# The forget tile in two buffers, loaded one head ahead, and one pool for the weight load buffers and attention's q, k, v rows

## The chip, the core and the metric

The kernel runs on one core of one Trainium2 chip. Its time is the device time of one launch in microseconds (us), as the median of several runs. On the core work TensorE (PE; its weight loads are shown apart as PEld), VectorE (DVE), ScalarE (ACT), GpSimd (POOL) and SyncE (SP), which here issues the transfers.

## What is computed

One layer of an encoder, for a prompt of 1024 rows and eight samples of 16 rows each with 256 cached rows. Width 1024, 8 heads of 64.

```python
x = x + 0.5 * gt1 * _swiglu(_modulate(x, g_ffn1, sh1, sc1), w_up1, w_down1)
# mixer: one projection z = h @ w_in, split into q, k, v, forget logits, u
q = _rms(q.reshape(B, T, N_HEADS, HEAD_DIM), g_q)
k = _rms(k.reshape(B, T, N_HEADS, HEAD_DIM), g_k)
logf = jax.nn.log_sigmoid((fl + b_f).astype(jnp.float32))
F = jnp.cumsum(logf, axis=1)
s = jnp.einsum('bqhd,bkhd->bhqk', q, k) * (HEAD_DIM ** -0.5)
s = s + (F_q[..., :, None] - F_k[..., None, :])      # -inf where k_pos > q_pos
o = softmax(s) @ v
y = jax.nn.silu(_layernorm(_dwconv(u_pad, conv_w, conv_b), conv_ln_g, conv_ln_b))
x = x + gt2 * (jnp.concatenate([o, y], axis=-1) @ w_out)
x = x + 0.5 * gt3 * _swiglu(_modulate(x, g_ffn2, sh3, sc3), w_up2, w_down2)
return _rms(x, g_final), states
```

## The kernel before

The stages follow one another: modulation vectors, first feed-forward block, combined projection, attention, output projection, second feed-forward block. All products are made of float32 values split into a high part `wh`/`hh` and a rest `wl`/`hl`, three matmuls each (lines 447 to 449 in the feed-forward blocks, 843 to 845 in the projection). Weights come in blocks of 512 KB: SP loads a block into a `raw` tile (a ring of 3), ACT casts it to `wh` (line 117), POOL or DVE subtracts for `wl` (line 118). The ring lies in the same pool as `wh` and `wl`, one pool for each stage.

**The projection** (lines 832 to 882) goes over six blocks of 256 columns (`cb` 0 and 1 are v, 2 and 3 are k, 4 and 5 are q) and in each over nine row tiles (`tt`: 8, the samples' rows, then 0 to 7), 24 matmuls into a bank `z` each. For k and q, ACT squares each of the four heads with a sum (line 859, written into a scratch tile `sq` that exists once), takes the root of the sums (line 860), and DVE makes the reciprocal `rr` (line 861). For `cb` 2 to 4 ACT copies the bank to the tile `qkv` (line 867), POOL multiplies it (line 868; for k once more by the gain), and SP stores it to the DRAM tiles `kd` or `qd` (line 875) and to the output; for `cb` 5 DVE multiplies straight out of the bank (line 865). The tiles `qkv` are slots of a ring of 4 (`tmp`), which the forget sums share (`nf`, line 792; `nfs`, line 810). Between the tiles DVE works through the taps of the depthwise convolution (lines 696 to 700).

**Attention** (from line 964) takes eight heads with four stages each, a stage being two query tiles of 128 rows, in the order 0, 2, 1, 3, the scores two stages ahead of the rest. Up to here PE's order is written out; in attention a scheduler sets the order on all engines from the code's order and the buffers. For each head, SP broadcasts a row of forget sums from DRAM to all partitions, tile `nfb`, 128x1024 (line 1214). For each query tile PE makes scores `s` (lines 1143 to 1146), DVE adds `nfb` and takes the minimum (`T`, `st`, line 1149), ACT takes the exponential (line 1150), DVE the reciprocal (line 1151), POOL scales (line 1152). PE transposes `T` into `pT` (line 251), ACT and DVE split that into `ph` and `pl` (lines 1170 and 1171), PE multiplies with the values `Vs` into `po` (line 1178), and DVE, then POOL, take the result through the tile `o32` (`o` in the profile) to `oth` and `otl` (lines 1190 to 1193). For each pair of heads SP loads 512 KB each of q, k and v rows back from DRAM (`qp`, `kp`, `vp`, line 1076); PE transposes them to `qT`, `kT`, and ACT, DVE and POOL make `Qs`, `Kh`, `kl`, `Vs` of them, for the next head's sake a head ahead. The samples' attention is woven in: `room` tiles hold a sample's cached keys and values (loads at lines 982, 985, 986, 996; the mask `sel`; PE's transposes `kTs`).

The forget tile has one buffer, and its load stands at a head's first stage:

```python
            if n % 4 == 0:
                nfb[h] = ap_.tile([P, SEQ], F32, tag="nfb", name="nfb", bufs=1)
                sp.dma_start(nfb[h], nfd[h:h + 1, :].to_broadcast([P, SEQ]))
                pieces = prep(h + 1) if h + 1 < H else []
```

SP issues transfers in the order of its queue: one that waits holds all behind it.

Of the kernel before, what the change touches and what calls it, by code (L numbers as in the profile page):

```python
# [8 lines left out]
F32 = mybir.dt.float32  # L9
# [34 lines left out]
def trunk_layer(  # L44
# [27 lines left out]
    def r32(ap):  # L72
        return ap.bitcast(F32)
# [21 lines left out]
    class Stream:  # L95
# [5 lines left out]
        def dma(self, n):  # L101
            while self.nd < min(n, self.limit):
                src, a, b = self.blocks[self.nd]
                t = self.pool.tile([P, WSL], F32, tag="raw", name="raw", bufs=3)
                v = t[:, :a * b].rearrange("p (a b) -> p a b", b=b)
                sp.dma_start(v, src)
                self.raw[self.nd] = t[:, :a * b]
                self.nd += 1
# [542 lines left out]
    mask_s = up_.tile([TS, H, TS], BF16, name="mask_s")  # L651
    sel = up_.tile([40, H, TS], F32, name="sel")
    qts = up_.tile([P, 4, P], F32, name="qts")
    kts = up_.tile([P, 4, P], F32, name="kts")
    pool_e.memset(mask_s, 0.0)
    pool_e.affine_select(out=mask_s, in_=mask_s, pattern=[[0, H], [1, TS]], compare_op=ALU.is_ge, fill=NEG, base=0, channel_multiplier=-1)
    pool_e.memset(sel, 0.0)
    pool_e.memset(sel[0:8], 1.0)
    pool_e.affine_select(out=sel[0:8], in_=sel[0:8], pattern=[[-1, H], [0, TS]], compare_op=ALU.is_equal, fill=0.0, base=0, channel_multiplier=1)
    for ct in range(4):  # L660
# [161 lines left out]
    def sample_t(cb):  # L822
# [6 lines left out]
        else:  # L829
            act.activation(dst, b[:, :256], AF.Copy, scale=gqc)  # L830

    for cb, (c0, n) in enumerate(QKV):
        i0 = b_qkv + 2 * cb
        w = [ws.take(i0 + kq) for kq in range(2)]
        ws.split(i0 + 4)
        for tt in [8] + list(range(8)):
# [18 lines left out]
            else:  # L855
                sq = up_.tile([P, DH], F32, tag="sq", name="sq", bufs=1)
                rr = up_.tile([P, 4], F32, tag="rr", name="rr", bufs=3)
                for h in range(4):
                    act.activation(sq, b[:, h * DH:(h + 1) * DH], AF.Square, accum_out=rr[:, h:h + 1])
                act.activation(rr, rr, AF.Sqrt, scale=1.0 / DH, bias=eps)  # L860
# [106 lines left out]
    mat, ap_ = open_pool("at", "left")  # L967
    room = [up_.tile([P, 1416], F32, tag=f"u{i}", name=f"room{i}") for i in range(4)]
    kc = room[0][:, :2 * DA].rearrange("p (a n) -> p a n", a=2)
# [9 lines left out]
    sfv = sf.rearrange("p (h t) -> p h t", h=H)  # L979

    def k_load(s):
        sp.dma_start(kc, cache_k[0, s].rearrange("(a p) h d -> p a (h d)", p=P))

# [4 lines left out]
    def s_a(s):  # L988
        if s == 0:
            k_load(0)  # L990
            dve.memset(nf, 1.0)
            pool_e.memset(bd, 0.0)
            pool_e.memset(vn, 0.0)
            pool_e.memset(pts[:, 256:], 0.0)
            dve.tensor_copy(sfv, sel)
        sp.dma_start(nf[0:H, :], nfsd[:, s, :])
# [72 lines left out]

    ld = {}  # L1070

    def a_load(p):
        ts = []
        for nm, src in (("qp", qd), ("kp", kd), ("vp", vd)):
            t = ap_.tile([P, 8, P], F32, tag=nm, name=nm)
            sp.dma_start(t, src[0:SEQ, p * P:(p + 1) * P].rearrange("(i t) n -> t i n", t=P))
            ts.append(t)
        ld[p] = ts

    nfb, Qs, Kh, Vs = {}, {}, {}, {}  # L1080
    a_load(0)
    kl_t = [ap_.tile([P, SEQ], F32R, tag=f"kl{i}", name=f"kl{i}") for i in range(2)]
# [102 lines left out]
    def out(h, j, po):  # L1185
        rows = slice(h % 2 * DH, (h % 2 + 1) * DH)
        t = tp.tile([P, C], F32, tag="rstd", name="ol", bufs=2)[:, :256]
        act.copy(t[:DH], po[DH:])
        o = ap_.tile([P, 256], F32, tag="o32", name="o32", bufs=2)
        dve.tensor_tensor(o[rows], po[:DH], t[:DH], ALU.add)  # L1190
        cols = slice(2 * j * P, (2 * j + 2) * P)
        pool_e.tensor_scalar(oth[rows, h // 2, cols], o[rows], 1.0, 1.0, ALU.mult, ALU.mult)
        pool_e.tensor_sub(otl[rows, h // 2, cols], o[rows], r32(oth[rows, h // 2, cols]))

# [166 lines left out]
```

## Time and profile before

| | |
|---|---|
| median of 3 runs | 2366.07 us (2365.07 to 2369.52) |
| profiled execution, its own time | 2364.53 us |
| its span in the profile | 2362.7 us |
| PE busy | 2300.0 us, 97% |
| DVE busy | 1242.5 us, 53% |
| ACT, POOL busy | 654.3 us, 533.0 us |
| the projection's last q tile leaves DVE | 1202.2 us after the start |
| forget tiles issued, heads 2 to 7 | 1246.65, 1271.56, 1294.86, 1316.33, 1339.17, 1360.93 us |

The profile is of one execution. A row of a timeline reads: start, length, engine, line, operation, out<-in, shape, and in brackets how long the engine was idle ahead of it and what ended that. A row of waits reads: who waited, for whom, us in total, times, the longest. A row of windows reads: from and to, length, then busy time and instructions of PE, PEld, DVE, ACT and POOL, the clock that TensorE was granted (1.00 is full), the share of the DMA engines, GB/s.

### The profile page before, as it was taken

How to read it: one execution, taken by the hardware profiler on the slowest of the kernel's cores; microseconds unless marked ns; L12 is line 12 of the kernel's file. 1: busy time of each engine (PE TensorE's matmuls, PEld its weight loads, DVE VectorE, ACT ScalarE, POOL GpSimd, SP SyncE). 2: the span in 40 equal slices, each digit the busy share in tenths (PEclk: the TensorE clock that was granted, in tenths of full speed). 3: DMA queues.
4: the chain of work that ended last, by engine and by line, in shares of the span. 5: the costliest groups of instructions: out<-in, count | busy, mean ns of one | idle time of the engine just before them, and what ended most of it. 6: DMA issues, size and time to landing. Idle time of an engine off the chain costs nothing.

```text
span 2362.7 us, 34229 instructions
## 1 busy us (share of the span) xinstructions
PE 2300.0 (97%) x13923; PEld 2205.2 (93%) x13923; DVE 1242.5 (53%) x2349; ACT 654.3 (28%) x1426; POOL 533.0 (23%) x423
## 2 busy tenths in 40 slices
PE   7999999999999998999989989999999999999998
PEld 4899999999999998999977779899999999999997
DVE  4542344244423448899978876843443344423445
ACT  4511111111111114314567753421111111111112
POOL 1111111211211211213446640121221221121210
PEclk8999999999999999999999999999999999999999
DMA  9432323311111111124233220111111111111102
GB/s 308 126 105 91 107 90 108 115 46 36 36 55 36 46 45 47 37 72 134 72 123 101 91 90 28 45 54 36 37 54 36 38 52 36 36 54 36 45 19 81
DMA packets 165301, 165.75 MB, mean 70 GB/s; under 512 B 9983, under 2 KB 141995, under 8 KB 162065
## 3 DMA queue, kind: packets, MB, share of 16 engines
q1 hardware_dynamic: 165145, 163.58, 22.3%
q8 instruction: 110, 1.80, 0.3%
q14 instruction: 46, 0.38, 0.1%
HBM read 147.10 MB, written 16.68 MB: 69 GB/s over the span
## 4 chain that ended last, share of the span: by engine, by line
PE 87%; DVE 7%; DMA 2%; ACT 2%; POOL 1%; issue 1%; SPq 0%; DVEq 0%; ACTq 0%; POOLq 0%
PE ub L447 9%; PE ub L448 9%; PE ub L449 9%; PE ua L447 8%; PE ua L448 8%; PE ua L449 8%; PE d L447 8%; PE d L449 8%; PE d L448 8%; PE pa L342 2%; DVE cv L699 2%; DMA nfb<-nfd 1%; PE z L843 1%; PE z L844 1%; PE z L845 1%; PE wo L449 1%
## 5 line engine op out<-in xcount | busy, mean ns | idle before, releaser
L118 POOL TENSOR_TENSOR wl<-raw,wh 128x1024 fp32r<-128x1024 f32 (+1 forms) x152 | 368.3, 2430 | 1592.2 <-ACT wh L117 1490.1
L486 DVE TENSOR_TENSOR g<-ub,sg 128x384 f32<-128x384 f32 x132 | 73.6, 558 | 772.8 <-PE ub L449 760.6
L447 PE MATMUL ub<-hh,wh 128*128 128x384 f32 x1168 | 399.0, 342 | 2.7 <-ACT hh L431 2.7
L448 PE MATMUL ub<-hl,wh 128*128 128x384 f32 x1168 | 397.5, 340 | 1.0 <-DVE hl L432 1.0
L449 PE MATMUL ub<-hh,wl 128*128 128x384 f32 x1168 | 397.3, 340 | 1.2 <-POOL wl L118 1.2
L447 PE MATMUL ua<-hh,wh 128*128 128x384 f32 x1136 | 381.9, 336 | 0.5 <-ACT hh L442 0.5
L448 PE MATMUL ua<-hl,wh 128*128 128x384 f32 x1136 | 379.9, 334 | 0.9 <-DVE hl L432 0.6
L449 PE MATMUL ua<-hh,wl 128*128 128x384 f32 x1136 | 379.9, 334 | 0.0
L117 ACT CAST wh<-raw 128x1024 fp32r<-128x1024 f32 (+1 forms) x160 | 165.8, 1050 | 763.2 <-issue 448.8
L454 DVE SCALAR_TENSOR_TENSOR x<-d,hgate,x 128x384 f32<-128x384 f32 (+1 forms) x528 | 296.1, 571 | 128.5 <-PE d L449 122.8
L447 PE MATMUL d<-gh,wh 128*128 128x384 f32 x1056 | 356.9, 338 | 4.8 <-DVE t L430 4.7
L449 PE MATMUL d<-gh,wl 128*128 128x384 f32 x1056 | 356.8, 338 | 0.0
L448 PE MATMUL d<-gl,wh 128*128 128x384 f32 x1056 | 355.9, 337 | 0.0
L447 PEld LDWEIGHTS ub<-hh,wh 128*128 128x128 f32 x1168 | 221.3, 189 | 13.1 <-issue 5.9
L447 PEld LDWEIGHTS ua<-hh,wh 128*128 128x128 f32 x1136 | 213.3, 188 | 11.8 <-issue 7.5
L448 PEld LDWEIGHTS ub<-hl,wh 128*128 128x128 f32 x1168 | 221.3, 189 | 1.7 <-DVE hl L432 1.7
L449 PEld LDWEIGHTS ub<-hh,wl 128*128 128x128 f32 x1168 | 221.2, 189 | 1.5 <-POOL wl L118 1.5
L448 PEld LDWEIGHTS ua<-hl,wh 128*128 128x128 f32 x1136 | 213.3, 188 | 1.5 <-DVE hl L432 0.9
L449 PEld LDWEIGHTS ua<-hh,wl 128*128 128x128 f32 x1136 | 213.3, 188 | 0.0
L447 PEld LDWEIGHTS d<-gh,wh 128*128 128x128 f32 x1056 | 199.1, 189 | 12.0 <-DVE t L430 5.0
L448 PEld LDWEIGHTS d<-gl,wh 128*128 128x128 f32 x1056 | 198.8, 188 | 0.0
L449 PEld LDWEIGHTS d<-gh,wl 128*128 128x128 f32 x1056 | 198.6, 188 | 0.0
(261 smaller groups left out, 3186.1 us busy)
## 6 DMA issues: line engine op xcount, KB each, us to landing
raw<-in_w_up_dram SPq DMA_DIRECT2D x88, 512.0 KB
araw<-in_w_ada_dram SPq DMA_DIRECT2D x24, 1024.0 KB
raw<-in_w_down_dram SPq DMA_DIRECT2D x44, 512.0 KB
raw<-in_w_in_dram SPq DMA_DIRECT2D x18, 512.0 KB
abulk<-in_w_ada_dram SPq DMA_DIRECT2D x12, 512.0 KB
out_dram<-yo SPq DMA_DIRECT2D x18, 256.0 KB
out_dram<-qkv SPq DMA_DIRECT2D x34, 128.0 KB
xin<-in_x_prompt_dram SPq DMA_DIRECT2D x8, 512.0 KB
```

The costliest lines, as they stand in the source:

```text
L117: act.copy(hi[:, :a * b], raw)
L118: self.sub.tensor_sub(lo[:, :a * b], raw, r32(hi[:, :a * b]))
L342: pe.matmul(pa[32 * i:32 * i + 32, :], lhsT=cst32[:, k, :], rhs=raw, start=first, stop=last)
L447: pe.matmul(out, lhsT=wh, rhs=mh_, start=first, stop=False)
L448: pe.matmul(out, lhsT=wh, rhs=ml_, start=False, stop=False)
L449: pe.matmul(out, lhsT=wl, rhs=mh_, start=False, stop=last)
L454: dve.scalar_tensor_tensor(xs[:, :n], b[:, :n], gate[:, dt, 0:1], xs[:, :n], ALU.mult, ALU.add)
L486: dve.tensor_tensor(g32, pb[:, :C], sg, ALU.mult)
L699: dve.scalar_tensor_tensor(cv if j < CW - 1 else acc[ct][:, :SEQ], u0, w, cv, ALU.mult, ALU.add)
L843: pe.matmul(b[:, :n], lhsT=a_h, rhs=wh, start=kt == 0, stop=False)
L844: pe.matmul(b[:, :n], lhsT=a_h, rhs=wl, start=False, stop=False)
L845: pe.matmul(b[:, :n], lhsT=a_l, rhs=wh, start=False, stop=kt == KD - 1)
```

## The change

The forget tile gets two buffers; head 0's is loaded ahead of the loop, head h+1's at head h's second stage (`nf_load`). The `raw` ring gets a pool of its own that stays open through the kernel, and attention's `qp`, `kp`, `vp` are tiles of that ring; the first pair's loads and the first sample's key load stand after row tile 2 of the projection's last block. The `sq` tile goes: squares are written into the tile's own slot `t`, which the copy or the product then overwrites. `sel`, `cl` and `o32` move into parts of other tiles, `o32` as one tile instead of two. What is in words only: `k_load` and `room[0]` move ahead of the projection loop with `a_load`, and the two instructions on `o32` after the first follow its new name.

```diff
-                t = self.pool.tile([P, WSL], F32, tag="raw", name="raw", bufs=3)
+                t = self.rawp.tile([P, WSL], F32, tag="raw", name="raw", bufs=3)
...
+    mraw, ws.rawp = open_pool("raw", "left")
     mw, wp = open_pool("w1", "left")
...
-    sel = up_.tile([40, H, TS], F32, name="sel")
-    pool_e.memset(sel, 0.0)
-    pool_e.memset(sel[0:8], 1.0)
-    pool_e.affine_select(out=sel[0:8], ...)
...
-    cl = up_.tile([P, PAST // P * NS * H], F32, tag="cl", name="cl")
+    cl = qts[:, 0, :]
...
+    def a_load(p):
+        ts = []
+        for nm, src in (("qp", qd), ("kp", kd), ("vp", vd)):
+            t = ws.rawp.tile([P, WSL], F32, tag="raw", name=nm, bufs=3)[:, :8 * P].rearrange("p (i n) -> p i n", n=P)
+            sp.dma_start(t, src[0:SEQ, p * P:(p + 1) * P].rearrange("(i t) n -> t i n", t=P))
...
-                sq = up_.tile([P, DH], F32, tag="sq", name="sq", bufs=1)
                 rr = up_.tile([P, 4], F32, tag="rr", name="rr", bufs=3)
                 for h in range(4):
-                    act.activation(sq, b[:, h * DH:(h + 1) * DH], AF.Square, accum_out=rr[:, h:h + 1])
+                    act.activation(t[:, h * DH:(h + 1) * DH], b[:, h * DH:(h + 1) * DH], AF.Square, accum_out=rr[:, h:h + 1])
...
+            if cb == 5 and tt == 2:
+                a_load(0)
+                k_load(0)
...
+    sel = room[3][:40, 1280:1280 + P].rearrange("p (h t) -> p h t", h=H)
+    o32 = room[3][:, 2 * P:4 * P]
...
         if s == 0:
-            k_load(0)
...
+            pool_e.memset(sel, 0.0)
+            pool_e.memset(sel[0:8], 1.0)
+            pool_e.affine_select(out=sel[0:8], ...)
...
-            t = ap_.tile([P, 8, P], F32, tag=nm, name=nm)
...
-    a_load(0)
+    def nf_load(h):
+        nfb[h] = ap_.tile([P, SEQ], F32, tag="nfb", name="nfb", bufs=2)
+        sp.dma_start(nfb[h], nfd[h:h + 1, :].to_broadcast([P, SEQ]))
+
+    nf_load(0)
...
-        o = ap_.tile([P, 256], F32, tag="o32", name="o32", bufs=2)
-        dve.tensor_tensor(o[rows], po[:DH], t[:DH], ALU.add)
+        dve.tensor_tensor(o32[rows], po[:DH], t[:DH], ALU.add)
...
             if n % 4 == 0:
-                nfb[h] = ap_.tile([P, SEQ], F32, tag="nfb", name="nfb", bufs=1)
-                sp.dma_start(nfb[h], nfd[h:h + 1, :].to_broadcast([P, SEQ]))
                 pieces = prep(h + 1) if h + 1 < H else []
+            if n % 4 == 1 and h + 1 < H:
+                nf_load(h + 1)
```

The instructions stay the same, but for one row on PE and one on POOL. Three places of the order, a row for each instruction with what it waits for (DMAHW is a transfer landed; x3 is three alike).

SP's queue at the projection's end, before: the q and k rows stand behind seven stores of the last block.

```order
L875 DMA qd<-qkv 128x256 [waits DMAHW7_49,DVE_49]
L1076 DMA qp<-qd 128x8x128 [waits DMAHW0_49]
L1076 DMA kp<-kd 128x8x128 [waits DMAHW1_49]
L875 DMA qd<-qkv 128x256 [waits DMAHW2_49,DVE_49]
L1076 DMA vp<-vd 128x8x128 [waits DMAHW3_49]
L982 DMA room_10605<-in_cache_k_dram 128x2x512 [waits DMAHW4_49,PE_49]
L1214 DMA nfb<-nfd 128x1024 [waits DMAHW5_49]
```

The same place after:

```order
L889 DMA qd<-qkv 128x256 [waits DMAHW6_49,Pool_49]
L835 DMA qp<-qd 128x8x128 [waits DMAHW4_49,DMAHW5_49,DMAHW3_49,DMAHW6_49,DMAHW2_49,DMAHW7_49,DMAHW1_49,DMAHW0_49]
L835 DMA kp<-kd 128x8x128
L835 DMA vp<-vd 128x8x128
L889 DMA qd<-qkv 128x256 [waits DVE_49,Activation_49]
```

The three loads stand ahead of all stores of the last block. Eight rows further on, ahead of that block's last store, the loads of the forget tiles of heads 0 and 1 now stand side by side, and wait for PE.

SP's queue around the load of head 3's forget tile, before (`room` rows are a sample's keys, forget sums, values and new values):

```order
L982 DMA room_10605<-in_cache_k_dram 128x2x512 [waits DMAHW5_49,PE_49]
L996 DMA room_10606<-nfsd 8x272 [waits DMAHW6_49,DMAHW3_49,PE_49]
L1076 DMA kp<-kd 128x8x128 [waits PE_49]
L1076 DMA vp<-vd 128x8x128 [waits Pool_49]
L985 DMA room_10606<-in_cache_v_dram 128x2x512 [waits DMAHW7_49,PE_49]
L1076 DMA qp<-qd 128x8x128 [waits PE_49]
L1214 DMA nfb<-nfd 128x1024 [waits DMAHW0_49,DVE_49]
```

After:

```order
L1001 DMA room_10575<-in_cache_v_dram 128x2x512 [waits DMAHW3_49,PE_49]
L1002 DMA room_10577<-vd 16x512 [waits DMAHW5_49,DMAHW1_49,PE_49]
L1092 DMA nfb<-nfd 128x1024 [waits DMAHW2_49,DVE_49]
L844 DMA room_10331<-in_cache_k_dram 128x2x512 [waits DMAHW6_49,PE_49]
L1014 DMA room_10575<-nfsd 8x272 [waits DMAHW7_49,DMAHW4_49,PE_49]
L835 DMA qp<-qd 128x8x128 [waits PE_49]
L835 DMA kp<-kd 128x8x128 [waits Pool_49]
```

The forget tile's load stood behind the third pair's rows; it now stands ahead of them and of a sample's keys, one head earlier.

ACT in the projection, two tiles of a q block, before:

```order
L859 ACTIVATE sq,rr<-z 128x64 [waits PE_49,Pool_49]
L859 ACTIVATE sq,rr<-z 128x64 [waits Activation_49] x3
L867 COPY qkv<-z 128x256 [waits DMAHW1_49,DMAHW0_49]
L860 ACTIVATE rr<-rr,eps 128x4 [waits Activation_49]
L859 ACTIVATE sq,rr<-z 128x64 [waits PE_49,Pool_49]
L859 ACTIVATE sq,rr<-z 128x64 [waits Activation_49] x3
L867 COPY qkv<-z 128x256 [waits DMAHW4_49,DMAHW2_49]
```

After:

```order
L873 ACTIVATE qkv,rr<-z 128x64 [waits DMAHW3_49,DMAHW0_49,DMAHW4_49,PE_49,Pool_49]
L873 ACTIVATE qkv,rr<-z 128x64 x3
L874 ACTIVATE rr<-rr,eps 128x4 [waits Activation_49]
L881 COPY qkv<-z 128x256
L873 ACTIVATE qkv,rr<-z 128x64 [waits DMAHW1_49,DMAHW2_49,PE_49,Pool_49]
L873 ACTIVATE qkv,rr<-z 128x64 x3
L874 ACTIVATE rr<-rr,eps 128x4 [waits Activation_49]
```

The wait for the slot's stores moved from the copy to the first square, the squares wait no more for one another, and the root now comes ahead of the copy.

More of the change, by code (lines that the diff above doesn't have):

```diff
@@ L656, in trunk_layer @@
     pool_e.affine_select(out=mask_s, in_=mask_s, pattern=[[0, H], [1, TS]], compare_op=ALU.is_ge, fill=NEG, base=0, channel_multiplier=-1)
-    pool_e.memset(sel, 0.0)
-    pool_e.memset(sel[0:8], 1.0)
-    pool_e.affine_select(out=sel[0:8], in_=sel[0:8], pattern=[[-1, H], [0, TS]], compare_op=ALU.is_equal, fill=0.0, base=0, channel_multiplier=1)
     for ct in range(4):
@@ L830, in sample_t, with k_load @@
             act.activation(dst, b[:, :256], AF.Copy, scale=gqc)
+    ld = {}
+    def a_load(p):
[3 more added lines that the diff above has]
+            sp.dma_start(t, src[0:SEQ, p * P:(p + 1) * P].rearrange("(i t) n -> t i n", t=P))
+            ts.append(t)
+        ld[p] = ts
+    room = []
+    def k_load(s):
+        if s == 0:
+            room.append(up_.tile([P, 1416], F32, tag="u0", name="room0"))
+        sp.dma_start(room[0][:, :2 * DA].rearrange("p (a n) -> p a n", a=2),
+                     cache_k[0, s].rearrange("(a p) h d -> p a (h d)", p=P))
     for cb, (c0, n) in enumerate(QKV):
@@ L967, in trunk_layer @@
     mat, ap_ = open_pool("at", "left")
-    room = [up_.tile([P, 1416], F32, tag=f"u{i}", name=f"room{i}") for i in range(4)]
+    room += [up_.tile([P, 1416], F32, tag=f"u{i}", name=f"room{i}") for i in range(1, 4)]
     kc = room[0][:, :2 * DA].rearrange("p (a n) -> p a n", a=2)
@@ L979, in trunk_layer @@
     sfv = sf.rearrange("p (h t) -> p h t", h=H)
-    def k_load(s):
-        sp.dma_start(kc, cache_k[0, s].rearrange("(a p) h d -> p a (h d)", p=P))
+    sel = room[3][:40, 1280:1280 + P].rearrange("p (h t) -> p h t", h=H)
+    o32 = room[3][:, 2 * P:4 * P]
     def v_load(s):
@@ L994, in s_a @@
             pool_e.memset(pts[:, 256:], 0.0)
+            pool_e.memset(sel, 0.0)
+            pool_e.memset(sel[0:8], 1.0)
+            pool_e.affine_select(out=sel[0:8], in_=sel[0:8], pattern=[[-1, H], [0, TS]], compare_op=ALU.is_equal, fill=0.0, base=0, channel_multiplier=1)
             dve.tensor_copy(sfv, sel)
@@ L1067, in sample_to @@
             f(s)
[L1070 to L1074, printed above, removed]
-            t = ap_.tile([P, 8, P], F32, tag=nm, name=nm)
-            sp.dma_start(t, src[0:SEQ, p * P:(p + 1) * P].rearrange("(i t) n -> t i n", t=P))
-            ts.append(t)
-        ld[p] = ts
     nfb, Qs, Kh, Vs = {}, {}, {}, {}
-    a_load(0)
+    def nf_load(h):
+        nfb[h] = ap_.tile([P, SEQ], F32, tag="nfb", name="nfb", bufs=2)
+        sp.dma_start(nfb[h], nfd[h:h + 1, :].to_broadcast([P, SEQ]))
+    nf_load(0)
     kl_t = [ap_.tile([P, SEQ], F32R, tag=f"kl{i}", name=f"kl{i}") for i in range(2)]
@@ L1188, in out @@
         act.copy(t[:DH], po[DH:])
-        o = ap_.tile([P, 256], F32, tag="o32", name="o32", bufs=2)
-        dve.tensor_tensor(o[rows], po[:DH], t[:DH], ALU.add)
+        dve.tensor_tensor(o32[rows], po[:DH], t[:DH], ALU.add)
         cols = slice(2 * j * P, (2 * j + 2) * P)
-        pool_e.tensor_scalar(oth[rows, h // 2, cols], o[rows], 1.0, 1.0, ALU.mult, ALU.mult)
-        pool_e.tensor_sub(otl[rows, h // 2, cols], o[rows], r32(oth[rows, h // 2, cols]))
+        pool_e.tensor_scalar(oth[rows, h // 2, cols], o32[rows], 1.0, 1.0, ALU.mult, ALU.mult)
+        pool_e.tensor_sub(otl[rows, h // 2, cols], o32[rows], r32(oth[rows, h // 2, cols]))
     def flush(n):
@@ L1325, in trunk_layer @@
     close_pool(mw)
+    close_pool(mraw)
     close_pool(mps)
```

## The prediction

> **What bounds the kernel now.** I read the page first: which engine is full, and what the chain of work that ended last consists of.
>
> ```profile
> span 2362.7 us, 34229 instructions
> PE 2300.0 (97%) x13923; PEld 2205.2 (93%) x13923; DVE 1242.5 (53%) x2349; ACT 654.3 (28%) x1426; POOL 533.0 (23%) x423
> PE 87%; DVE 7%; DMA 2%; ACT 2%; POOL 1%; issue 1%; SPq 0%; DVEq 0%; ACTq 0%; POOLq 0%
> PE ub L447 9%; PE ub L448 9%; PE ub L449 9%; PE ua L447 8%; PE ua L448 8%; PE ua L449 8%; PE d L447 8%; PE d L449 8%; PE d L448 8%; PE pa L342 2%; DVE cv L699 2%; DMA nfb<-nfd 1%; PE z L843 1%; PE z L844 1%; PE z L845 1%; PE wo L449 1%
> ```
>
> PE is 97% busy, and the two feed-forward blocks, which the change does not touch, are most of the chain. What the change can win is PE's idle time and time at a low clock. One transfer has a share of the chain: the forget tile's. So the second view is the chain itself, with start and length of each step. Five of the eight forget tile loads stand on it (the first and the last are shown), and ahead of them the load of the k rows:
>
> ```profile
> 1200.23 5.25 DMA kp<-kd
> ...
> 1246.65 6.01 DMA nfb<-nfd
> 1271.56 7.33 DMA nfb<-nfd
> ...
> 1360.93 5.42 DMA nfb<-nfd
> ```
>
> A transfer on the chain costs only what an engine waits for it. The waits of the attention stretch give DVE's part (times, longest at the end), and PE's timeline gives the idle time in brackets ahead of the matmuls that came late:
>
> ```profile
> DVE T L1149 <- DMA nfb<-nfd: 7.3, 5, 2.1
> ```
> ```profile
> 1202.35 0.45 PE L251 MATMUL kTs<-ident,room 128*128 128x128 f32 x1 [2.15 <-DVE qkv L865]
> 1205.53 0.42 PE L251 MATMUL kT<-ident,kp 128*64 128x128 f32 x1 [2.09 <-DMA kp<-kd]
> 1253.04 0.39 PE L1143 MATMUL s<-Kh,Qs 128*128 128x256 f32 x1 [1.84 <-DVE st L1149]
> 1279.27 0.39 PE L1143 MATMUL s<-Kh,Qs 128*128 128x256 f32 x1 [1.64 <-DVE st L1149]
> 1323.59 0.39 PE L1143 MATMUL s<-Kh,Qs 128*128 128x256 f32 x1 [1.18 <-DVE st L1149]
> 1344.61 0.38 PE L1143 MATMUL s<-Kh,Qs 128*128 128x256 f32 x1 [0.79 <-DVE st L1149]
> 1366.73 0.39 PE L1143 MATMUL s<-Kh,Qs 128*128 128x256 f32 x1 [1.12 <-DVE st L1149]
> ```
>
> The link is this. The single forget tile is free when T of the old head's last scores has read it; its load is issued then (1246.65) and takes 6.01; DVE stops at the new head's first T, the score bank stays taken, and PE, which runs ahead of DVE, stops at the next scores (1253.04). That happens in five heads.
>
> The third view is the windows from one forget tile's issue to the next (length, then busy time of PE, PEld, DVE, ACT, POOL, the granted clock, DMA share, GB/s), and below them some clock windows:
>
> ```profile
> 1246.65:1271.56 24.91, 22.68 (x178) 18.27 (x177) 19.47 (x51) 17.94 (x42) 15.01 (x25) 0.93 0.32 102
> 1271.56:1294.86 23.30, 20.90 (x170) 16.34 (x168) 17.55 (x48) 17.08 (x42) 14.38 (x25) 1.00 0.33 99
> 1294.86:1316.33 21.47, 21.06 (x178) 17.03 (x177) 19.68 (x52) 17.30 (x42) 15.03 (x25) 1.00 0.36 121
> 1339.17:1360.93 21.76, 20.57 (x172) 16.51 (x171) 19.33 (x52) 16.85 (x41) 14.48 (x25) 1.00 0.23 75
> ```
> ```profile
> 1205.70:1209.12 3.42, 3.42 (x17) 2.49 (x16) 1.61 (x4) 1.84 (x3) 1.29 (x3) 0.50 1.11 362
> 1253.49:1256.90 3.41, 3.41 (x18) 3.08 (x17) 3.01 (x11) 2.49 (x7) 1.23 (x3) 0.50 0.00 0
> 1280.90:1284.30 3.40, 3.40 (x24) 2.16 (x23) 3.34 (x10) 1.75 (x5) 1.30 (x5) 1.00 0.00 0
> ```
>
> The head from 1294.86 has no such gap, and takes 21.47 with PE busy for 21.06. The others are that plus their gap (23.30 − 1.64 = 21.66), and the one from 1246.65 also ran 3.41 us at half clock behind its gap.
>
> **The change part by part.** *Two forget tiles, loaded a head ahead.* As many loads as before, no new instruction. Head h+1's load is issued after the first of head h's four stages, about three quarters of 21.5 = 16 us ahead of its use, and the longest load is 7.33, so 9 us are left over. It stands ahead of other rows in SP's queue and waits for DVE's last T of head h−1, which is over by then, so it holds nothing behind it. The gaps go: 1.84 + 1.64 + 1.18 + 0.79 + 1.12 = 6.57. Next late after the forget tile is DVE itself: 19.68 busy in the 21.47 of the gapless head, under PE's 21.06, so I take all 6.57; bounds 3.3 (half goes into DVE, which loses the idle time in which its queue drained) and 6.57.
>
> *The clock.* The stretch at 1253.49 worked 3.41 us at 0.50, so it lost 3.41 × 0.5 = 1.7. Without the 1.84 gap ahead of it I take the whole 1.7; bounds 0 and 1.7. The trace says that the link is no rule: 1.84 idle was followed by 0.50, 1.64 idle (at 1279.27) by 1.00. The Trainium skill ("TensorE: Matmul & The Clock Gate", Part 1: The HAM clock gate) has the clock fall only after an idle window of about 3.4 us; this trace differs, since no gap here was that long and two stretches were at 0.50. By the page no clock time hangs on these gaps.
>
> *q, k, v rows for the first pair, and the first sample's keys, loaded from the last projection block on.* The rows were in a pool that opens with attention, where the kp load ended on the chain and PE idled 2.09. Now they use the weight load buffers, free when the last projection weights are split. The loads wait for the fourth block's q stores, whose last is in SP's queue at 1183.66; at 362 GB/s (the clock row at 1205.70, when these loads run) 1.5 MB take 4.3 us, so even doubled they are in by 1195, ahead of 1205.53. Until the fourth block's stores have landed, the last block's stand behind this wait on SP, and the ring's tiles and with them ACT wait for those; but the two stores of that row span 6.20, so about 6 us lie between the blocks, room for a landing, and I take 0.
>
> ```profile
> 1183.66 6.20 SPq L875 DMA_DIRECT2D qd<-qkv  x2
> 1361.79 36.71 SPq L106 DMA_DIRECT2D raw<-in_w_out_dram  x7
> 1390.06 2.94 ACT L117 CAST wh<-raw 128x1024 fp32r<-128x1024 f32 x3
> ```
>
> So 2.09 goes, and DVE's and POOL's work on these rows comes earlier with it. What is next late there is the sample's kTs gap (2.15). The half-clock stretch at 1205.70 stands behind both; with one gap of 1.85 left, between the 1.84 that was followed by 0.50 and the 1.64 that wasn't, it can go or stay: 0.4, bounds 0 and 1.7. The price of sharing the ring is at the other end: the output projection's weights wait until the last pair's rows have been read, and stand behind the last sample's value load. They were issued at 1361.79 and cast at 1390.06, 28 us of cover, one head's length: nothing.
>
> *Squares into the output tile.* The scratch tile of the squares was single, so each square waited for the one before on its own engine. Now they don't, but the first waits for the ring's slot (four tiles), which so far only the copy behind them waited for. The projection's window, the waits for stores in it, and the rows of one k tile and of the last tile:
>
> ```profile
> 1137.00:1200.00 63.00, 62.49 (x527) 62.03 (x525) 57.10 (x110) 36.98 (x208) 22.79 (x33) 1.00 0.19 61
> ```
> ```profile
> ACT qkv L867 <- DMA kd<-qkv: 4.7, 2, 2.5
> ```
> ```profile
> 1145.76 0.37 ACT L867 COPY qkv<-z 128x256 f32<-128x256 f32 x1 [2.51 <-DMA kd<-qkv]
> 1146.02 0.30 ACT L860 ACTIVATE rr<-rr,eps 128x4 f32<-128x4 f32 x1
> 1149.40 0.16 DVE L861 RECIPROCAL rr<-rr 128x4 f32<-128x4 f32 x1
> ...
> 1199.79 0.22 ACT L859 ACTIVATE sq<-z 128x64 f32<-128x64 f32 x1 [1.17 <-PE z L845]
> 1200.14 0.22 ACT L859 ACTIVATE sq<-z 128x64 f32<-128x64 f32 x1
> ...
> 1201.51 0.18 DVE L861 RECIPROCAL rr<-rr 128x4 f32<-128x4 f32 x1 [2.16 <-ACT rr L860]
> ```
>
> A square each 0.35 us (1200.14 − 1199.79): where the slot is late, four squares, 1.4, and the copy's place, 0.3, put the root up to 1.7 later. It ended at 1146.32, and its reciprocal ran at 1149.40 because DVE had convolution taps ahead: 3.08 of cover, so the step costs 0. Without the cover each tile's later root would lengthen the slot's circle (a rival, below). At the last tile DVE waits for the root and PE for DVE (the 2.15 gap), so a quicker row of squares is worth something: with the 0.35 step down to the square's own 0.22, 4 × 0.13 = 0.5 at most; I take 0.3, bounds 0 and 0.5.
>
> *Moved tiles.* The selection mask's three instructions move on POOL from before the projection into the first sample step, near the projection's end. POOL is busy there for 22.79 of 63.00: 0; should what POOL waits for there come earlier, they would hold the fills and value tiles behind them. The attention output's scratch is one tile instead of two, but two consecutive heads use different rows of it, so a wait needs the same head's next turn. The nearest is at the end:
>
> ```profile
> 1385.24 0.74 POOL L1193 TENSOR_TENSOR otl<-o,oth 64x256 fp32r<-64x256 f32 x1
> 1386.94 0.42 DVE L1190 TENSOR_TENSOR o<-po,ol 64x256 f32<-64x256 f32 x1
> ```
>
> POOL is done at 1385.98, 0.96 ahead of the next write: 0. If that cover goes, DVE waits and with it the bank po.
>
> **The sum.** 6.57 + 1.7 + 2.09 + 0.4 + 0.3 = 11.1. The profiled execution took 2364.53 (its span is 2362.7), so 2353.5; the median of the runs is 2366.07, 1.54 above that execution, so 2355.0. By the rows alone; by the skill's page the sum would be 9.0.
>
> **Rivals.**
> - *The clock stays.* For it: the two gaps of 1.84 and 1.64 with different clocks, so that something other than the gap decides. Against it: both half-clock stretches of attention's first heads stand behind gaps. Both clock terms are 0: 11.1 − 2.1 = 9.0, median 2357.1. Its rule is the one that the skill's page would give.
> - *The stall passes on.* DVE, kept from waiting, comes to the same place 1 us later with all its work: for it, 19.47 busy in the head from 1246.65, 78% of its length; against it, the gapless head. Half of 6.57, no clock there: 3.3 + 2.09 + 0.3 = 5.7, median 2360.4.
> - *The load isn't earlier in time.* SP takes its rows in order; the forget tile's stands behind value loads that wait for PE. If these come as late as the old issue, only the start wins: 2.09 + 0.4 + 0.3 = 2.8, median 2363.3. Against it: 9 us of reserve.
> - *More than the gaps.* PE's ends are modelled, so its 21.06 may hold waits that earlier T's take out; the heads' PE busy time varies down to 20.57. With 0.9 (21.47 − 20.57) more in each of eight heads: 7.2 on top, median 2347.8.
> - *Slower: the ring of slots.* In the projection PE does a tile of 24 matmuls in 2.87 us, from its window (63.00 / 527 × 24), so a slot's circle (squares, copy, POOL's products, store, landing) has 11.5 us. Two copies in this stretch waited for stores, so the circle of the k tiles is near it, and the squares now lie inside it. Each us beyond 11.5 costs a quarter us a tile, 9 us over 36 tiles; over all four blocks it turns the sum from 1.8 us on (11.1 + 4.7 = 15.8), and with 2.0 it gives 11.1 − 18 = −6.9, median 2373.0. Against it: the squares add 1.7 at most, and 3.08 of DVE's cover lie ahead.
>
> **How the numbers follow.** Chances: the forecast 0.46, clock stays 0.10, passes on 0.15, load not earlier 0.10, more 0.12, ring 0.07. A measurement of this kernel tells about 0.2%, 4.7 us, from no change: faster is below 2361.3, slower above 2370.8. Faster: the forecast, the clock's case, the larger gain, and 0.09 of the stall passing on, in all 0.77. Same: the rest of that and the late load, 0.16. Slower: the ring, 0.07. The forecast's own range is 2352 to 2358, by its bounds (the start's clock 1.7 instead of 0.4 and the last squares at 0.5 below; no clock at the start, half of the other, no gain at the squares above, and 1.5 for the runs' scatter, whose lowest is 1.0 below the median, with each). The range to hold the time 8 times in 10 reaches from 2349, inside the larger gain, to 2363, inside the late load; half of each of these two and the ring, 0.18, stay outside.
>
> **What would show it.** Right: no wait of DVE's T for the forget tile, no gap over 0.5 us ahead of the scores at a head's start, heads of 21 to 22 us, no gap ahead of kT, and the projection as long as now with PE at 62.5 of 63.0. The clock row behind the third head's start tells the clock's case, a gap ahead of the scores that names DVE with DVE's queue full tells the stall passing on, and the time of the forget tile's issue tells the late load. Wrong: PE gaps ahead of z, with squares that wait for stores; a wait of the first T for its forget tile, which now starts with another beside it; or a new gap at the output projection's weights.

## The result

| | median us | lowest to highest | ratio to before, 95% interval |
|---|---|---|---|
| before, 4 runs | 2367.78 | 2365.07 to 2369.52 | |
| changed, 4 runs | 2353.06 | 2349.94 to 2354.46 | 0.994 (0.9928 to 0.9952) |
| changed again, beside the experiments (before there: 2367.26), 5 runs | 2350.66 | 2350.13 to 2355.37 | 0.9932 (0.9919 to 0.9946) |

The kernel is 0.6% faster, some 15 us. The forecast was 2355.0, from 2349 to 2363. The profiled execution of the changed kernel took 2352.19, against 2364.53 before. Its page begins:

```profile
span 2350.5 us, 34254 instructions
PE 2298.0 (98%) x13923; PEld 2205.7 (94%) x13923; DVE 1243.5 (53%) x2349; ACT 644.3 (27%) x1426; POOL 534.4 (23%) x423
```

The view of the forget tile (its loads, and what DVE waited for ahead of T): the wait for the load is gone, and only PE's scores are left.

```profile
L1092 SPq DMA_DIRECT2D nfb<-nfd x8: 332/401/447, 1203.2 to 1332.7; - x8
its engine sat idle before it (us, times) until:
  PE s L1159: 3.1, 7
```

To see where the time went I cut both profiles at the same four instructions of PE. The windows are the projection (first to last z matmul), attention's start (to the first sample's transpose sOT), its heads (to the first wo, the output projection's matmul) and the output projection. Columns as before; first the kernel before, then the changed one.

```profile
1035.81:1199.76 163.95, 160.30 (x1340) 158.64 (x1340) 158.29 (x266) 80.10 (x385) 55.45 (x64) 1.00 0.33 100
1199.76:1229.08 29.32, 22.23 (x162) 16.57 (x161) 21.29 (x57) 20.34 (x50) 15.77 (x25) 0.88 0.58 180
1229.08:1391.16 162.08, 149.19 (x1210) 119.08 (x1208) 131.63 (x352) 122.49 (x291) 101.27 (x165) 0.99 0.30 92
1391.16:1501.16 110.00, 108.16 (x599) 105.31 (x599) 82.22 (x135) 44.20 (x63) 16.63 (x14) 0.98 0.16 48
```
```profile
1038.73:1203.55 164.82, 161.33 (x1340) 160.01 (x1340) 159.25 (x268) 71.23 (x385) 54.17 (x63) 0.94 0.36 109
1203.55:1230.76 27.21, 21.66 (x163) 16.17 (x161) 22.38 (x56) 19.55 (x50) 18.72 (x28) 0.89 0.48 156
1230.76:1382.60 151.84, 145.51 (x1210) 118.72 (x1208) 132.01 (x352) 122.15 (x291) 101.25 (x165) 0.95 0.30 95
1382.60:1489.64 107.04, 106.28 (x599) 103.98 (x599) 81.52 (x136) 44.97 (x65) 17.77 (x13) 0.95 0.17 50
```

So: projection +0.9, start −2.1, heads −10.2, output projection −3.0. The first feed-forward block, ahead of all of it, was 2.9 later in this one execution (1038.73 against 1035.81). Outside its half-clock windows this one profile reads a clock of 0.95 where the others read 1.00; its matmuls of 128x384 in the feed-forward blocks take 0.33 us as before, so I don't count that as a slower clock.

At attention's start one half-clock window went. Before, the stretch that the prediction shows from 1205.70 on had begun a window earlier, at 1202.29, so it was 6.83 long; in this execution one window is left (first row: before).

```profile
1202.29:1205.70 3.41, 1.26 (x5) 0.89 (x6) 3.38 (x7) 0.00 (x0) 0.00 (x0) 0.50 1.17 320
1206.56:1209.97 3.41, 2.86 (x13) 2.19 (x14) 3.38 (x7) 0.64 (x2) 3.33 (x5) 0.50 0.51 192
```

The gap for the k rows is gone, but the gap ahead of the second kTs group grew from 2.15 to 3.08, and PE now waits for POOL's copy of Kh:

```profile
1207.08 0.45 PE L252 MATMUL kTs<-ident,room 128*128 128x128 f32 x1 [3.08 <-DVE qkv L879]
1212.53 0.39 PE L1156 MATMUL s<-Kh,Qs 128*128 128x256 f32 x1 [1.39 <-POOL Kh L1117]
```

DVE's timeline says why the first grew: a layer norm add stands between the last reciprocal and its product, and takes 1.62 where an add of the same shape took 0.55 shortly before. POOL's subtraction runs at that time, and its next rows say why Kh is late (last three lines): it has the zeros under kl and head 1's value tile to make first. Before, the zeros were done at 1200.88 and the first copy of Kh began at 1207.29.

```profile
1202.64 0.55 DVE L911 TENSOR_TENSOR lna<-acc,acc 128x384 f32<-128x384 f32 x1
...
1204.88 0.18 DVE L875 RECIPROCAL rr<-rr 128x4 f32<-128x4 f32 x1 [1.10 <-ACT rr L874]
1204.98 1.62 DVE L911 TENSOR_TENSOR lna<-acc,acc 128x384 f32<-128x384 f32 x1
1206.52 0.41 DVE L879 TENSOR_TENSOR qkv<-z,rr 128x256 f32<-128x256 f32 x1
```
```profile
1204.92 1.26 POOL L1132 TENSOR_TENSOR Vs<-vp,Vs 128x512 fp32r<-128x512 f32 x1
1206.27 3.46 POOL L1100 TENSOR_SCALAR kl<-zt 64x512 fp32r<-64x512 f32 x4
...
1211.86 1.19 POOL L1117 TENSOR_SCALAR Kh<-Kh 64x512 fp32r<-64x512 f32 x2
```

### The profile page after: what moved, and what is told of

Its sections match the earlier page's. It is cut to its first block, busy times and chain, and to the rows that moved or that the text cites. A ratio compares the mean times of both kernels' runs of the same rounds, so it can differ in the third digit from the quotient of the medians.

```text
span 2350.5 us, 34254 instructions
## 1 busy us (share of the span) xinstructions
PE 2298.0 (98%) x13923; PEld 2205.7 (94%) x13923; DVE 1243.5 (53%) x2349; ACT 644.3 (27%) x1426; POOL 534.4 (23%) x423
## 4 chain that ended last, share of the span: by engine, by line
PE 43%; DVE 3%; ACT 2%; issue 1%; POOL 1%; DMA 0%; DVEq 0%; ACTq 0%; POOLq 0%; SPq 0%
PE ub L449 4%; PE ub L450 4%; PE ub L448 4%; PE d L450 4%; PE d L449 4%; PE d L448 4%; PE ua L450 4%; PE ua L448 4%; PE ua L449 4%; PE wo L448 1%; PE wo L449 1%; PE wo L450 1%; PE po L1191 1%; PE pT L252 1%; ACT T L1163 1%
## 5 line engine op out<-in xcount | busy, mean ns | idle before, releaser
L448 PEld LDWEIGHTS d<-gh,wh 128*128 128x128 f32 x1056 | 199.3, 189 | 12.3 <-DVE t L431 5.0
```

The source lines that it names most:

```text
L448: pe.matmul(out, lhsT=wh, rhs=mh_, start=first, stop=False)
```

## The experiments

All were compared with the kernel before, five rounds each. Two variants needed no run: with the first pair's loads written at their old place, or with two forget tiles whose load is written at the head's own first stage, the built programs have the same order as the changed kernel (in the first case on all engines, in the second on PE, DVE and SP). The shared ring and the second buffer make the loads early, not the lines moved in the code.

**One forget tile** (the rest of the change alone).

```diff
-        nfb[h] = ap_.tile([P, SEQ], F32, tag="nfb", name="nfb", bufs=2)
+        nfb[h] = ap_.tile([P, SEQ], F32, tag="nfb", name="nfb", bufs=1)
...
-    nf_load(0)
...
             if n % 4 == 0:
+                nf_load(h)
...
-            if n % 4 == 1 and h + 1 < H:
-                nf_load(h + 1)
```

> The changed kernel with one forget tile again, its load written at the head's first stage; the shared ring, the squares and the moved tiles stay. My theory (the forget tile's gaps are most of the gain): five or so gaps of 0.8 to 1.8 us ahead of a head's scores come back, with DVE's T waiting for the forget tile, so 7 to 9 of the 13 to 15 us go and 3 to 6 us of gain stay, a ratio to the kernel before of 0.9975 to 0.999. Rival (the earlier rows and the quicker squares, or a clock that happened to stay up, made the gain): the ratio stays at 0.994 to 0.9955.

Measured: 2360.41, ratio 0.9971 (0.996 to 0.9983). Its waits, the heads and the output projection, and two gaps:

```profile
DVE T L1161 <- DMA nfb<-nfd: 8.6, 5, 2.7
```
```profile
1227.75:1390.38 162.63, 150.35 (x1209) 119.92 (x1207) 132.10 (x352) 122.36 (x291) 101.23 (x165) 0.98 0.29 90
1390.38:1497.34 106.96, 106.20 (x599) 103.93 (x599) 81.49 (x135) 44.24 (x63) 16.86 (x13) 1.00 0.16 50
```
```profile
1252.25 0.58 PE L1155 MATMUL s<-Kh,Qs 128*128 128x256 f32 x1 [2.35 <-DVE st L1161]
1278.37 0.39 PE L1155 MATMUL s<-Kh,Qs 128*128 128x256 f32 x1 [1.64 <-DVE st L1161]
```

The head gaps are back and the heads take 162.6 as before, so the heads' gain is the forget tile's. But 6.9 us of gain stayed (2367.26 − 2360.41), a little more than the 3 to 6 that I expected, and less than the rival's, which had the ratio at 0.9955 at most. In the profiled execution 3.0 of it are in the output projection, which nobody had on the list.

**The forget tile alone** (the kernel before, with two forget tiles; scratch and mask moved for room).

```diff
...
+    nf_load(0)
...
-        o = ap_.tile([P, 256], F32, tag="o32", name="o32", bufs=2)
+        o = o32
...
-                nfb[h] = ap_.tile([P, SEQ], F32, tag="nfb", name="nfb", bufs=1)
-                sp.dma_start(nfb[h], nfd[h:h + 1, :].to_broadcast([P, SEQ]))
...
+            if n % 4 == 1 and h + 1 < H:
+                nf_load(h + 1)
```

> The kernel before with two forget tiles, loaded a head ahead; for room the output scratch and the mask move as in the change. q, k, v rows keep tiles of their own, the squares their scratch. My theory: the head gaps go as in the changed kernel and the gap of about 2 us for the first k rows stays, so 8 to 10 us faster than before, ratio 0.9957 to 0.9967. Rival (the rest of the change made the gain): at most 4 us faster, ratio 0.998 or more. If the two parts are independent, this gain and that of the kernel with one forget tile add up to the whole.

Measured: 2352.59, ratio 0.9938 (0.9925 to 0.995).

```profile
1037.46:1201.19 163.73, 161.30 (x1340) 160.00 (x1340) 157.84 (x266) 80.13 (x385) 56.12 (x66) 0.99 0.33 101
1201.19:1229.41 28.22, 22.45 (x161) 16.68 (x160) 21.79 (x57) 19.86 (x50) 15.90 (x25) 0.88 0.65 204
1229.41:1380.86 151.45, 144.61 (x1210) 118.03 (x1208) 132.00 (x352) 121.72 (x291) 101.41 (x165) 1.00 0.30 95
1380.86:1490.84 109.98, 108.15 (x599) 105.30 (x599) 82.17 (x135) 44.15 (x63) 16.63 (x13) 0.98 0.16 48
```
```profile
1206.96 1.06 PE L251 MATMUL kT<-ident,kp 128*64 128x128 f32 x4 [2.56 <-DMA kp<-kd]
```

The heads lose 10.6 here, the output projection nothing; the k rows' gap stays, as expected. The gain was larger than I expected: in the profiled executions 10.6, and 14.7 between medians, since the profiled execution of before (2364.53) lies 2.7 below the median of the ten runs beside it (2367.26), and the one of this kernel (2353.9) 1.3 above its own. Between medians the two parts' gains (14.7 and 6.9) are 5.0 more than the whole (16.6); the first offset, counted once too often, is 2.7 of that. Stage by stage, in the profiled executions, they add up for the projection, the heads and the output projection within 0.2 us. At the start they don't: −1.1 and −3.1 alone, against −2.1 together.

**The changed kernel again.**

> The changed kernel once more, as the mark for the others on the same chip: ratio 0.993 to 0.995. In its first profile the half-clock stretch behind the output projection's first wait (1.41 us, in both kernels) was missing, and the feed-forward block ahead was 2.9 us later. Theory that both are chance: in this profile the stretch can be there, and the feed-forward block ends within 1 us of that of before. Rival (both belong to the change): they show again as in the first profile.

Measured: 2350.66, ratio 0.9932 (0.9919 to 0.9946); five runs at 2350.13, 2350.32, 2350.66, 2354.95 and 2355.37. The feed-forward block was 0.7 late instead of 2.9: that was chance. The output projection took 106.83 again: that belongs to the change. The profiled execution was the one of 2354.95. Its projection, start and heads:

```profile
1036.53:1201.60 165.07, 160.28 (x1340) 158.63 (x1340) 159.51 (x268) 71.00 (x385) 54.22 (x63) 1.00 0.36 109
1201.60:1232.93 31.33, 24.44 (x162) 17.79 (x160) 22.46 (x56) 19.53 (x50) 18.71 (x28) 0.84 0.45 136
1232.93:1384.28 151.35, 144.52 (x1209) 118.11 (x1207) 131.88 (x352) 121.87 (x291) 101.35 (x165) 1.00 0.31 95
```
```profile
1203.36:1206.77 3.41, 1.50 (x12) 1.26 (x12) 3.38 (x5) 0.55 (x3) 3.32 (x4) 1.00 0.87 283
1206.78:1210.19 3.41, 1.22 (x8) 0.72 (x8) 3.31 (x6) 1.88 (x4) 3.16 (x5) 1.00 0.61 154
1210.19:1220.43 10.24, 9.85 (x39) 6.48 (x40) 4.77 (x17) 4.75 (x10) 3.27 (x9) 0.50 0.18 53
```

Three windows of 3.41 at half clock, where the first profile has one and the kernel before two, and a start of 31.3 in place of 27.2: in such an execution the start's gain of 2 is a loss of 2. These 4.1 would be most of the 4.7 between this run and those at 2350; none of those was profiled. The projection, which has no half-clock window here and none before (the first profile of the changed kernel has one, from 1073.44), took 1.1 longer than before.

**Written order at the output projection.** In the changed kernel the layer norm's total lnb stands ahead of the first matmul that needs wl; before, PE waited there (first row: before).

```profile
1392.41 0.45 PE L449 MATMUL wo<-oth,wl 128*128 128x384 f32 x1 [0.46 <-DVE wl L118]
```
```profile
1383.41 0.82 PE L928 MATMUL lnb<-lna,ones 128*128 128x384 f32 x2
1383.86 0.55 PE L450 MATMUL wo<-oth,wl 128*128 128x384 f32 x1
```
```diff
-                if (n, d2, c) == (0, 1, 0):
+                if (n, d2, c) == (0, 0, 0):
```

> The changed kernel with one edit: PE's written order begins at the output projection's first group instead of its second, so the layer norm's total lnb no longer stands ahead of the first matmul that needs wl, and PE waits for wl as in the kernel before. Both kernels wait 1.40 us for wh ahead of it. Theory (a window of 3.41 us with more than about 1.7 us of idle PE is followed by one at half clock): 1.4 plus a wait of 0.5 to 0.9 for wl fall into one window, the next is at 0.50, and the output projection takes about 110 us as before instead of 107, 2 to 3 us slower than the changed kernel. Rival (the 3 us came from the weights or the layer norm's adds, not from the order): the same time as the changed kernel within 1 us, and clock 1.00 there.

Measured: 2354.86, ratio 0.9949 (0.9936 to 0.9961), 4.2 slower than the changed kernel. In its profiled execution:

```profile
1385.45 0.44 PE L450 MATMUL wo<-oth,wl 128*128 128x384 f32 x1 [0.64 <-DVE wl L118]
```
```profile
1201.49:1232.78 31.29, 24.39 (x162) 17.75 (x160) 22.46 (x56) 19.54 (x50) 18.77 (x28) 0.84 0.43 132
1384.19:1492.05 107.86, 106.45 (x599) 103.87 (x599) 81.58 (x135) 44.31 (x63) 16.88 (x14) 1.00 0.16 49
```

The wait is back, and with it 1.0 of the 3.0; the half clock isn't (1.00), as the two waits fell into two windows. So the order is a part of the 3.0, and that the rest is the half-clock window (which before and the forget tile alone had there, and no kernel with the ring had) is likely but not shown. Much of the 4.2 is a start with three half-clock windows, which the edit doesn't touch: its five runs (2354.39 to 2355.48) lie where the changed kernel's two runs at 2354.95 and 2355.37 do. So the 1.0 is shown in the stage, and not in the whole time.

**Only the last tile's squares in scratch.**

```diff
-                    act.activation(t[:, h * DH:(h + 1) * DH], b[:, h * DH:(h + 1) * DH], AF.Square, accum_out=rr[:, h:h + 1])
+                    act.activation(sq if last else t[:, h * DH:(h + 1) * DH], b[:, h * DH:(h + 1) * DH], AF.Square, accum_out=rr[:, h:h + 1])
```

> The changed kernel with one edit: only the last tile of the projection squares into a scratch tile again, so its four squares take about 1.26 instead of 0.84 us, but the scheduler then sets DVE's last product straight behind the reciprocal, with the layer norm's first adds after it, as in the kernel before. Theory (the add between reciprocal and product, 1.63 us while POOL subtracts, made the first gap 3.08 instead of the 1.7 that quicker squares should give): the gap ahead of the second kTs group falls to 2.1 to 2.2. Rival (the squares' place is what counts): it grows to 3.5. In time 0 to 1 us faster than the changed kernel, or up to 3 if a half-clock window goes.

Measured: 2351.45, ratio 0.9933 (0.992 to 0.9945).

```profile
1205.07 0.41 PE L252 MATMUL kTs<-ident,room 128*128 128x128 f32 x2 [2.16 <-DVE qkv L881]
```

As the theory had it: slower squares, and the gap falls from 3.08 to 2.16, since the add is out of the way (the product begins 0.27 behind the reciprocal, at 1204.50, and the adds follow it). In time, the same as the changed kernel.

**All squares in scratch**, and **the same with ACT's zeros** (the last two lines of the diff are the second kernel's alone).

```diff
+                sq = up_.tile([P, DH], F32, tag="sq", name="sq", bufs=1)
...
-                    act.activation(t[:, h * DH:(h + 1) * DH], b[:, h * DH:(h + 1) * DH], AF.Square, accum_out=rr[:, h:h + 1])
+                    act.activation(sq, b[:, h * DH:(h + 1) * DH], AF.Square, accum_out=rr[:, h:h + 1])
...
-            pool_e.tensor_scalar(kl_t[i][DH:, hf * 512:(hf + 1) * 512], zt[DH:], 1.0, 1.0, ALU.mult, ALU.mult)
+            act.copy(kl_t[i][DH:, hf * 512:(hf + 1) * 512], zt[DH:])
```

> The changed kernel with the squares' scratch tile back in every tile; ring, forget tiles and moved tiles stay. What the runs so far point to: with the squares in the slot, the projection's last matmul came 0.9 to 1.1 us later against its first than in the kernel before (gaps of 1.2 and 1.4 ahead of z at the tiles that share the slots with the forget sums), and the layer norm's add stood ahead of the last product. Theory (the squares' part of the change costs by itself): the projection is 1 us shorter, the first gap 2.15, so 1.5 to 2 us faster than the changed kernel, 2348.5 to 2349.5. Rival (the slot's squares pay): 0.3 to 1 us slower, with the gaps ahead of z as they are.

> The same with the zeros under kl written by ACT instead of POOL. Theory (POOL's copy of Kh behind the zeros is a second gap at the start): no gap over 0.5 us ahead of the first scores, 0.5 to 1 us less than with the scratch alone, about 2348, ratio 0.992, and all runs within 2 us, since too little idle is left at the start for more than one half-clock window. Rival (ACT's four casts hold the copy of kTs and the first Kh): the same time as with the scratch alone.

Measured: 2352.65 (0.9935, 0.9921 to 0.9949; four runs from 2352.34 to 2352.94 and one of 2347.85), and 2350.91 (0.9935, 0.9923 to 0.9948). Projection and start of the two:

```profile
1036.52:1200.21 163.69, 161.26 (x1340) 159.96 (x1340) 157.79 (x266) 80.12 (x385) 54.43 (x63) 0.99 0.37 110
1200.21:1231.35 31.14, 25.51 (x166) 18.23 (x164) 23.98 (x59) 20.11 (x51) 18.28 (x28) 0.84 0.43 130
```
```profile
1037.19:1200.94 163.75, 161.30 (x1340) 160.01 (x1340) 157.85 (x266) 80.25 (x385) 54.42 (x63) 0.99 0.37 110
1200.94:1229.28 28.34, 22.21 (x162) 16.09 (x160) 22.47 (x57) 22.02 (x54) 15.54 (x24) 0.88 0.47 149
```

The projection is 1.1 shorter with the scratch, as before the change: squares in the slot cost that. My times were missed, since the start took it back: three and two half-clock windows.

**The start: last product on ACT, zeros on ACT** (the zeros by the same edit as just above).

```diff
-                if cb == 5:
+                if cb == 5 and tt == 7:
+                    for h in range(4):
+                        act.activation(t[:, h * DH:(h + 1) * DH], b[:, h * DH:(h + 1) * DH], AF.Copy, scale=rr[:, h:h + 1])
+                elif cb == 5:
```

> The changed kernel with two edits at attention's start: the last q tile's product goes to ACT, which scales the four heads, so that the layer norm's add that the scheduler put between DVE's reciprocal and product no longer stands ahead of the bank's release; and ACT instead of POOL writes the zeros under kl, so that POOL's copy of Kh isn't behind 3.5 us of fills. Theory (the changed kernel's gaps of 3.08 and 1.39 us at the start are on the path): the first falls to about 2.1, the second under 0.5, 1.5 to 2 us faster than the changed kernel, ratio about 0.9935. Rival (what PE gains there it waits for DVE a stage later): same time as the changed kernel within 0.5 us.

Measured: 2349.76, ratio 0.9925 (0.9913 to 0.9938), five runs within 2349.28 to 2351.24.

```profile
1204.99 1.12 PE L252 MATMUL kTs<-ident,room 128*128 128x128 f32 x4 [3.01 <-ACT qkv L880]
```
```profile
1201.55:1227.86 26.31, 21.53 (x161) 15.86 (x160) 22.70 (x55) 22.83 (x58) 15.76 (x24) 0.94 0.51 161
```

The second gap went, the first did not: two of the zero casts stood ahead of the scaling on ACT. It has the lowest median (a kernel below has the same), and no run above 2352; against the changed kernel the intervals overlap.

**The banks turned**, with the zeros on ACT and without.

```diff
+        if cb == 5:
+            for _ in range(2):
+                dve.memset(bank("skip")[:1, :1], 0.0)
```

> The changed kernel with two edits: two one-element writes turn the ring of eight score banks by two ahead of the last block, so that the last z bank isn't one that attention's first transposes take; and ACT writes the zeros under kl instead of POOL. Theory (the start's gap of 3 us is the wait for the last z bank alone): no gap over 0.6 us between the projection's last matmul and the first scores but for a DVE or ACT wait for Kh or Qs, no or one half-clock window there, 3 to 5 us faster than the changed kernel, ratio about 0.992. Rival (the transposes run early and their readers, ACT and DVE, are the bound, so PE waits at the scores instead): the idle time moves to the scores, at most 1 us faster.

> The changed kernel with the ring of banks turned alone, the zeros still POOL's. Theory: the gap of 3 us ahead of the second kTs group goes, but the scores then wait longer for POOL's copy of Kh, which stands behind 3.5 us of zeros and the value tiles: 2 to 3 us of idle at the first scores, 0 to 2 us faster than the changed kernel. Rival (POOL's copy is early enough): as fast as the kernel with both edits.

Measured: 2351.24 (0.9935, 0.9921 to 0.9948) and 2350.01 (0.9936, 0.9922 to 0.9949). The theory fell: the first kTs group now waits, and longer, 3.48 in both (shown: with the zeros on ACT).

```profile
1204.67 0.66 PE L252 MATMUL kTs<-ident,room 128*128 128x128 f32 x2 [3.48 <-ACT kl L1103]
```

**PE kept busy in the gap** (16 transposes that nothing reads), in the changed kernel and in the kernel with the edited start.

```diff
+            if cb == 5 and tt == 7:
+                f = bank("fill")
+                for i in range(16):
+                    T(f[:, i % 4 * P:(i % 4 + 1) * P], ident)
```

> The changed kernel with 16 transposes of the identity behind the projection's last matmul, 2.4 us of PE work that nothing reads, in the gap of 3.1 us ahead of the second kTs group; the order on all other engines is the same row for row. They take no wait away, so PE's useful work can start no earlier. Theory (idle PE in a window of 3.41 us brings the half clock): idle in the gap falls to 0.7, at most one half-clock window is left at the start where there were one or three, and the kernel is 1.7 us faster than the changed kernel's fast executions and 5 faster than its slow ones, all runs within 2 us near 2348. Rival (the half clock comes with the load of the stage, or the gap only costs its length): same clock, same time, or 0.5 slower.

> The same 16 transposes in the kernel whose last q tile is scaled by ACT and whose zeros ACT writes, which had no second gap at the start. Theory: no window with more than 1.6 us of idle at the start, so clock 1.00 through attention's start, 1.7 us faster than that kernel without them, about 2348, ratio 0.992. Rival: as that kernel, 2349.8, with its one half-clock window.

Measured: 2353.7 (0.994, 0.9928 to 0.9953) and 2349.76 (0.9928, 0.9915 to 0.9942). The starts of the two, and the half-clock stretch of the first:

```profile
1200.84:1232.11 31.27, 26.11 (x178) 19.45 (x176) 22.45 (x56) 19.71 (x50) 18.78 (x28) 0.84 0.43 135
1209.23:1219.47 10.24, 9.63 (x38) 6.29 (x39) 4.72 (x16) 4.54 (x9) 3.28 (x9) 0.50 0.21 54
```
```profile
1201.65:1228.00 26.35, 22.20 (x178) 16.86 (x176) 22.70 (x55) 22.79 (x58) 15.96 (x24) 1.00 0.50 163
```

In the first the forecast fell, though not the link between idle time and clock. The transposes took 1.91, so 1.36 of the gap stayed, and behind it the gaps of 1.32 and 1.41, as in the changed kernel, left 2.12 of idle in the next window. Three half-clock windows followed, and two of the five runs were at 2350.3 and 2350.5, the others at 2353.7 to 2354.8. In the second the clock stayed at 1.00 all through the start, as expected, and it gained nothing: 26.35 against 26.31. So the one half-clock window there had cost nothing; that ACT and DVE set the pace (without the transposes 22.8 and 22.7 busy, PE 21.5) is likely, but not shown.

One thing shows only over all runs. Of the 24 of the four kernels with two forget tiles, the squares in the slot and POOL's zeros (the changed kernel, the written order, the banks turned without ACT's zeros, the filled gap), 14 took over 2353.5; of the 20 of the four kernels whose zeros ACT writes, none did. The two with turned banks differ in the zeros alone: two runs of five over 2354 with POOL's, none over 2353 with ACT's. That points to the wait for Kh behind POOL's zeros as the source of the longer runs; five runs each don't show it.

## Why the prediction was right, and where it wasn't

- *The forget tile.* Right in mechanism, and 1.9 short in size. The stretch of the heads lost 10.2 (forecast: 6.57 + 1.7 = 8.3), and 10.7 in the second profile. PE's idle time there fell from 162.08 − 149.19 = 12.89 to 151.84 − 145.51 = 6.33, by 6.56; in the second profile by 6.06. That the first comes within 0.01 of the forecast's 6.57 is luck. PE's busy time fell by 3.68: 1.7 for the half-clock window at 1253.49, and 2.0 that was in no gap (3.0 in the second). That is the rival "more than the gaps", with a quarter to two fifths of its 7.2. The bound "half goes into DVE" was not touched. What these 2 to 3 us are stays open: in the modelled ends, or in the new order.
- *The shared ring.* The k rows' gap went, as forecast. But the start as a whole gave 2.1 in one profiled execution of the changed kernel and cost 2.0 in the other, where the sum had 2.8 (2.09 + 0.4 + 0.3). Two steps failed. "What is next late there is the sample's kTs gap (2.15)" left out POOL: vp, early too, lets it make head 1's value tile ahead of Kh's copy, and the zeros now stand there as well. And "the half-clock stretch at 1205.70 … can go or stay: 0.4" misread the stretch, which had two windows and began at 1202.29, before the k rows' gap. It neither went nor stayed: it had one window in one execution and three in the other. A window can cost up to 1.7 (half of 3.41, an estimate), so this can be most of both the −2.1 and the +2.0.
- *Squares into the slot.* "3.08 of cover, so the step costs 0" failed: the tile that I priced had cover, others hadn't, and PE waits ahead of z where forget sums share the slots. Before, it waited there 0.93 (at 1127.84, ahead of the window that the prediction looked at) and 0.51 for a reciprocal; in the first profile of the changed kernel 1.32 (below), in the second 1.19 and 1.40. Cost: 0.9 and 1.1 in the projection, 1.1 against the scratch. That is the slower rival's mechanism, at a small part of its 18 us. The other half, "a quicker row of squares: 0.3", was right on ACT (the last root came 1.30 behind the last z matmul, against 1.73 with the scratch) and turned round on DVE, by an add that the order of the changed program already showed in that place.

```profile
1142.50 0.35 PE L858 MATMUL z<-wh,hh 128*128 128x256 f32 x1 [1.32 <-DVE nfs L807]
```

- *The output projection.* No term had it: 3.0, with every kernel that has the ring. "Nothing", which I gave to the ring's other end, was right of the weights' cover and wrong of the order behind it.
- *The sum* came out close, −12.3 in the profiled executions against −11.1, and in part by luck: 1.9 more in the heads, 3.0 at the output projection and 0.7 behind it stand against the squares' 0.9, the start's 0.7 and the 2.9 of the late feed-forward block.

## What to carry to other kernels

Where a single buffer's load stands on the chain, sum PE's gaps behind it, and take them all if the load can be issued two load times ahead of its use (here some 16 us, with 7.33 for the longest load): that sum was right to half a us. Then read the order of the changed program at each place where something comes early, because a scheduler fills the place with other work, and what it puts between a reciprocal and the product that frees a bank can cost more than the edit gains. Two buffers in one pool were enough here to make the scheduler load ahead; where the line stood in the code changed nothing.

## What the runs showed of the hardware

**The clock follows idle time in windows.** The half-clock stretches of all 14 profiles begin on a grid of 3.41 us. From the projection to the second feed-forward block, a window at full clock with at most 1.43 us of idle PE was never followed by one at 0.50; with 1.94 or more it always was, 35 of 35; between 1.59 and 1.92, in 6 of 13. So the same gap costs a window at half clock or not by where it falls on the grid, and a second gap close by can add windows. Of the 41 half-clock stretches there, 19 had one window, with at most 0.58 of idle PE in it, and 17 had two, with 0.72 or more in the first. Five had three: there the window ahead of the one that brought the half clock had 1.36 to 1.91 of idle already, in the other 36 cases at most 0.67. All five are at attention's start, which would fit runs of one program 4 to 5 us apart. Why the clock does so stays open. The Trainium skill ("TensorE: Matmul & The Clock Gate", Part 1: The HAM clock gate) names the window of about 3.4 us, free-running, and the trace agrees; it asks for a whole idle window, and here a little more than half of one was enough.

**DVE and POOL slow each other.** The add of 128x384 took 0.55 alone and 1.62 beside POOL's subtraction of 1.26, which had begun 0.06 ahead of it. With only the last tile's squares in scratch an add began 0.08 ahead of the same subtraction (1204.84 and 1204.92): that add kept its 0.55, the subtraction took 1.60, and the next add 1.63. So the one that comes second seems to be held; these are a few cases. The Trainium skill ("GPSIMD Engine Reference", section 1, Specifications) says that POOL shares its interfaces to SBUF with DVE, with contention for DVE instructions with two SBUF inputs; the trace agrees.
